# A hybrid two-layer trunk on one core: plain granules moved among the seven-product sets of its feed-forward parts

## The chip, the cores and the metric

The kernel runs on one core of a Trainium2 chip. The metric is the device time of one execution in microseconds (us); the kernel before took 1269.57 us, the median of three runs between 1269.21 and 1272.35. One core has a matrix engine (TensorE, PE in the profile), a vector engine (VectorE, DVE), a scalar engine (ScalarE, ACT), GpSimd (POOL) and SyncE (SP), which here issues loads. Each works through its own list of instructions in order; semaphores tie the lists together, and DMA queues bring the weights from memory.

## The reference

A trunk of two layers over 256 tokens of width 1024, in float32. What is computed, cut to what matters here:

```python
h = x
for i in range(2):
    h = h + 0.5 * swiglu(rmsnorm(h, ffn1_norm[i]), ffn1_w_gate[i], ffn1_w_up[i], ffn1_w_down[i])
    hn = rmsnorm(h, mix_norm[i])
    h = h + (diff_attention(hn, ...) if i == 0 else ssd_mixer(hn, ...))
    h = h + memory_cross_attention(rmsnorm(h, xa_norm[i]), mem, ...)
    h = h + 0.5 * swiglu(rmsnorm(h, ffn2_norm[i]), ffn2_w_gate[i], ffn2_w_up[i], ffn2_w_down[i])
return rmsnorm(h, final_norm)

def swiglu(h, w_gate, w_up, w_down):
    return (jax.nn.silu(h @ w_gate) * (h @ w_up)) @ w_down
```

The four `swiglu` calls are the feed-forward parts (FFNs); the change touches them alone. The gate and up weights are 1024 by 2816, the down weight 2816 by 1024. The attention of layer 0 needs tables of cosines and sines of the positions (the rope tables), which the kernel works out during the first FFN.

## The kernel before, in words

**Products.** Every float32 operand of a matmul is split into two parts, a rounded high part and the rest, and a product takes three matmuls: high by high, high by low, low by high. Lines 262, 263 and 264 are these three (`mm3`). An operand of weights is split one **granule** at a time, two rows of 128 by 512 columns: ACT casts the high part (`whi`, line 224), DVE subtracts to get the low part (`wlo`, line 225). Four buffers each hold `whi` and `wlo`. The weights come as tiles of 1 MB (4 times 128 rows by 512 columns) in eight buffers; their loads stand in SP's queue. Granules are split a fixed number of granules ahead of their use, so the order in which they are used is also the order of splits on ACT and DVE and of loads on SP.

**An FFN.** The hidden width of 2816 is cut into chunks of 512, numbered 0 to 4, and a half chunk 5. Chunk 0 and the half chunk (gate and up side by side, tiles named `gateup`) are plain products, and in the first FFN chunk 1 too. The others are **sets**: gate and up of a chunk, for both halves of the tokens, as seven products of sums in place of eight plain ones. With b11 and b21 the upper and lower half of the up weight of the chunk and b12 and b22 those of the gate, the seven are, in the order in which PE does them: x1 = b11 + b12, b11, x2 = x1 + b22, b22, x3 = b12 + b22, b21, x4 = x2 + b21. The sums x1 and x2 are made by DVE (`Sum`, line 203, one instruction over a whole tile); x3 and x4 by DMAs of POOL's queue that add into a tile. The left operands are sums of token blocks (`s_hi`, `s_lo`, made by lines 481 and 486 from `sraw`). The seven results are collected in three banks of PSUM, so a product that adds onto a bank must wait until the result before has been read or moved: line 830 (`c12`, its tile is named p) reads the bank that b22's product has filled, before x3's product may go on in it; line 835 (`c22`) does the like after b21's product, and line 841 takes the two products with the up results.

**Order.** A product is two granules, 6 matmuls each. Between the products stand **hosts**: plain granules of 12 matmuls (half chunk, plain chunks, down products of earlier chunks). The lists `five`, `six`, `eight` and `ten` say how many hosts stand ahead of each of the seven products of a set; `share` deals them out and `weave` makes the one list. After each chunk the hidden values are transposed by PE (line 854, `htp`) and split into `hid_hi` by ACT and `hid_lo` by DVE (line 858).

**The down product** has two halves of 512 output columns. Its `d0` and `d1` granules up to chunk 3 are hosts. What is left stands at the end: `d0[7:]`, of half 0 (chunk 3's second granule, chunk 4's two), then the tail of half 1 (chunks 3 and 4, two granules each). `fin` updates h with the finished half and starts the next norm. In the last FFN a function of its own (`last`) does the tail by token blocks, and half 0's evaluation goes with it. Up chunks end in line 804 (`up_fin`), which also calls what else hangs on that chunk: after chunk 1 of the first FFN the rope tables (lines 735 to 771, some forty small DVE instructions).

PE, DVE, ACT and SP follow the written order only for the first two units of the program; later a scheduler orders the lists, from the order in which the program names the work.

Of the kernel before, what the change touches and what calls it, by code (L numbers as in the profile page):

```python
# [57 lines left out]
def trunk(ctx, tc, a, out):  # L58
# [81 lines left out]
    pipe = Pipe()  # L140
    units = []
# [260 lines left out]
    def weave(steps):  # L402
        def run(*gr):
            for g, (_, f) in zip(use(gr), steps):
                f(g)
        units.append(([g for g, _ in steps], run))

    def down(src, half, ks, lhs, banks, first, last):

        def step(g):  # L410
            if not banks:
                banks.extend(acc("out") for _ in range(2))
            for k in range(g.nk):
                kt = g.k0 + k
                for t in range(2):
                    xh, xl = pipe.need(lhs, kt)
                    ts = slice(t * P, (t + 1) * P)
                    mm3(banks[t], xh[:, ts], xl[:, ts], g.hi[:, k, :], g.lo[:, k, :], kt == first, kt == end)
                    pipe.pe(0.68)
                if kt == end:  # L420
                    last(half, banks)
        end = ks[-1][0] + ks[-1][1] - 1 if last else -1
        return [(Gran(k, 2, (w, 0, 512)), step) for w in [W(src, k0, nk, half * 512, 512) for k0, nk in ks]
                for k in range(w.k0, w.k0 + w.nk, 2)]
# [350 lines left out]
        nc.scalar.activation(sin.rearrange("p t f -> p (t f)"), tot, AF.Sin)  # L775


    def ffn_hidden(nm, l, norm, fin, extra=None):
        hid = [None] * NHT
        box = {}  # L780

# [80 lines left out]
        wide([(wg, 0, 512)], norm, "gate", gate_fin(0), **({} if units else dict(single=True, eng=nc.gpsimd)))  # L862
        c = HID // 512
        half = stream([(wg, c * 512, 256), (wu, c * 512, 256)], norm, "gateup", up_fin(c, 256, 256))
        five, six = [1, 0, 1, 0, 1, 1, 1], [1, 1, 1, 0, 1, 1, 1]
        eight, ten = [2, 1, 1, 1, 1, 1, 1], [2, 1, 2, 1, 2, 1, 1]
        if norm is first_norm:
            wide([(wu, 0, 512)], norm, "up", up_fin(0))
            n = half + stream([(wg, 512, 512)], norm, "gate", gate_fin(1)) + stream([(wu, 512, 512)], norm, "up", up_fin(1))
            counts = {2: eight, 3: eight, 4: ten}  # L870
        else:
            n = stream([(wu, 0, 512)], norm, "up", up_fin(0)) + half
            counts = {1: six, 2: five, 3: six, 4: five}
        wd = a[nm + "_w_down"][l]
# [10 lines left out]
        steps = []  # L885
# [2 lines left out]
            steps += share(n[:sum(k)], s, k)  # L888
            n = n[sum(k):]
        assert not n  # L890
        weave(steps + d0[7:])
        return hid, wd

    def ffn(nm, l, norm, nxt, extra=None):
        fin = upd(0.5, nxt)
        hid, wd = ffn_hidden(nm, l, norm, fin, extra)
        weave(down(wd, 1, [(12, 4), (16, 4)], hid, [], 12, fin))


    def diff_attention(norm, nxt, kv):  # L900
# [627 lines left out]
    def last(norm):  # L1528
# [7 lines left out]
                nc.gpsimd.dma_start(fn[c], a["vec"][352 + c * 512:352 + (c + 1) * 512].partition_broadcast(P))  # L1536


        def mms(o, t, g, k, cs, kt, start, stop):
            xh, xl = pipe.need(hid, kt)  # L1540
            ts = slice(t * P, (t + 1) * P)
            mm3(o, xh[:, ts], xl[:, ts], g.hi[:, k, cs], g.lo[:, k, cs], start, stop)
            pipe.pe(0.68 * (cs.stop - cs.start) / 512)
# [33 lines left out]
        def first_half(half, banks):  # L1577
            for t in range(2):
                for q in range(2):
                    evac(banks[t][:, q * 256:(q + 1) * 256], t, q)  # L1580
        hid, wd = ffn_hidden("ffn2", 1, norm, first_half, {12: final_gain})
        banks = {}

        def run(*gr):
            ready(gr[-1].at + AHEAD)
            last_ = gr[-1].k0 + gr[-1].nk == 20
            for t, c0, c1 in [(0, 0, 512), (1, 0, 256), (1, 256, 512)]:
# [7 lines left out]
                if last_:  # L1595
                    for q in range((c1 - c0) // 256):
                        evac(b[:, q * 256:(q + 1) * 256], t, 2 + c0 // 256 + q)
        ws = [W(wd, k, 4, 512, 512) for k in (12, 16)]
        gr = [Gran(k, 2, (w, 0, 512)) for w in ws for k in (w.k0, w.k0 + 2)]
        units.append((gr[:1], run))  # L1600
        units.append((gr[1:], run))


# [71 lines left out]
```

## Time and profile before

| | |
|---|---|
| median of three runs (lowest to highest) | 1269.57 us (1269.21 to 1272.35) |
| the profiled execution's own time | 1269.06 us |
| its span | 1267.2 us |
| PE busy | 1251.8 us, 99% |
| DVE busy | 1057.7 us, 83% |
| ACT busy | 878.6 us, 69% |
| granted PE clock, mean over the span | 0.997 |
| DMA moved | 213 GB/s on average |

The span runs from the first to the last recorded instruction; the execution's own time has 1.9 us around it. Matmuls are pipelined: a row's own duration is longer than the distance between two starts, so the distance of starts tells how fast PE goes. A row of the timeline has the start, the time to the end of the last instruction of the row, the engine, the line, the operation, what it writes and reads, its shape and how often in a row; in brackets the idle time ahead of it and what ended that. A row of the windows has the window, its length, the busy time (and count) of PE, DVE, ACT, POOL and the weight loads in the order PE, weight load, DVE, ACT, POOL, then the granted clock, the share of DMA and GB/s.

### The profile page before, as it was taken

How to read it: one execution, taken by the hardware profiler on the slowest of the kernel's cores; microseconds unless marked ns; L12 is line 12 of the kernel's file. 1: busy time of each engine (PE TensorE's matmuls, PEld its weight loads, DVE VectorE, ACT ScalarE, POOL GpSimd, SP SyncE). 2: the span in 40 equal slices, each digit the busy share in tenths (PEclk: the TensorE clock that was granted, in tenths of full speed). 3: DMA queues.
4: the chain of work that ended last, by engine and by line, in shares of the span. 5: the costliest groups of instructions: out<-in, count | busy, mean ns of one | idle time of the engine just before them, and what ended most of it. 6: DMA issues, size and time to landing. Idle time of an engine off the chain costs nothing.

```text
span 1267.2 us, 18142 instructions
## 1 busy us (share of the span) xinstructions
PE 1251.8 (99%) x6751; PEld 1070.5 (84%) x6751; DVE 1057.7 (83%) x1451; ACT 878.6 (69%) x1394; POOL 161.6 (13%) x139
## 2 busy tenths in 40 slices
PE   9999999999999999999999999999999999999997
PEld 6788888788998888887878889999998898888886
DVE  6989777886787898888998976788999887899886
ACT  6676764686676876766776856777776766877773
POOL 1111002111100011000111000022222200011100
PEclk9999999999999999999999999999999999999999
DMA  9977975335786698985899976665544686489971
GB/s 333 277 234 204 352 242 167 133 123 159 208 243 167 169 257 254 265 284 167 235 229 257 281 263 195 207 199 167 178 155 134 170 247 186 162 235 266 259 221 34
DMA packets 158315, 269.79 MB, mean 213 GB/s; under 512 B 6889, under 2 KB 43410, under 8 KB 158226
## 3 DMA queue, kind: packets, MB, share of 16 engines
q1 hardware_dynamic: 137744, 229.75, 53.2%
q0 software_dynamic: 19744, 38.28, 17.9%
q8 instruction: 53, 0.87, 0.3%
q10 hardware_dynamic: 738, 0.59, 0.1%
q14 instruction: 36, 0.29, 0.1%
HBM read 267.52 MB, written 1.08 MB: 212 GB/s over the span
## 4 chain that ended last, share of the span: by engine, by line
PE 87%; DVE 7%; issue 2%; DMA 2%; ACT 2%; POOL 0%; POOLq 0%; DVEq 0%; ACTq 0%
PE out L264 9%; PE out L263 8%; PE out L262 8%; PE seven L262 8%; PE seven L263 7%; PE seven L264 7%; DVE wlo L225 3%; PE xs L264 2%; DMA w<-in_ffn_w_gate_dram 2%; PE xs L262 2%; PE xs L263 2%; PE mk L262 1%; PE xq L263 1%; PE mk L264 1%; PE xq L264 1%
## 5 line engine op out<-in xcount | busy, mean ns | idle before, releaser
L225 DVE TENSOR_TENSOR wlo<-w,whi 128x1024 fp32r<-128x1024 f32 (+2 forms) x532 | 642.4, 1219 | 141.6 <-ACT whi L224 131.6
L224 ACT CAST whi<-w 128x1024 fp32r<-128x1024 f32 (+2 forms) x534 | 552.6, 1041 | 270.5 <-PE out L264 104.0
L264 PE MATMUL out<-whi,hid_lo 128*128 128x512 f32 x336 | 131.2, 391 | 0.9 <-DVE hid_lo L858 0.9
L263 PE MATMUL out<-wlo,hid_hi 128*128 128x512 f32 x336 | 131.3, 391 | 0.0
L262 PE MATMUL out<-whi,hid_hi 128*128 128x512 f32 x336 | 130.8, 394 | 0.0
L262 PE MATMUL seven<-whi,s_hi 128*128 128x512 f32 x272 | 107.9, 397 | 1.8 <-DVE p L830 1.8
L263 PE MATMUL seven<-wlo,s_hi 128*128 128x512 f32 x272 | 106.1, 390 | 0.4 <-DVE wlo L225 0.4
L264 PE MATMUL seven<-whi,s_lo 128*128 128x512 f32 x272 | 106.1, 390 | 0.0
L203 DVE TENSOR_TENSOR w<-w 128x2048 f32<-128x2048 f32 x32 | 73.2, 2286 | 6.3 <-DMA w<-in_ffn_w_gate_dram 6.2
L264 PEld LDWEIGHTS out<-whi,hid_lo 128*128 128x128 f32 x336 | 63.0, 188 | 15.0 <-DVE hid_lo L858 2.0
L199 POOL DMA_DIRECT2D w<-in_ffn_w_up_dram x30 | 36.5, 1233 | 305.9 <-DVE wlo L225 304.8
L263 PEld LDWEIGHTS out<-wlo,hid_hi 128*128 128x128 f32 x336 | 63.1, 188 | 13.8 <-DVE wlo L225 1.2
L262 PEld LDWEIGHTS out<-whi,hid_hi 128*128 128x128 f32 x336 | 63.1, 188 | 12.5
L263 PE MATMUL seven<-wlo,xh 128*128 128x512 f32 x180 | 70.4, 391 | 1.9 <-DVE wlo L225 1.9
L264 PE MATMUL seven<-whi,xl 128*128 128x512 f32 x180 | 70.4, 391 | 0.0
L262 PE MATMUL seven<-whi,xh 128*128 128x512 f32 x180 | 70.3, 391 | 0.0
L199 POOL DMA_DIRECT2D w<-in_ffn_w_gate_dram x30 | 36.9, 1467 | 227.7 <-DVE w L203 98.4
L262 PEld LDWEIGHTS seven<-whi,s_hi 128*128 128x128 f32 x272 | 51.1, 188 | 13.7 <-DVE p L830 3.9
L264 PEld LDWEIGHTS seven<-whi,s_lo 128*128 128x128 f32 x272 | 51.1, 188 | 10.8
L263 PEld LDWEIGHTS seven<-wlo,s_hi 128*128 128x128 f32 x272 | 51.1, 188 | 10.4 <-DVE wlo L225 0.8
L263 PEld LDWEIGHTS seven<-wlo,xh 128*128 128x128 f32 x180 | 33.9, 189 | 9.4 <-DVE wlo L225 2.3
L264 PEld LDWEIGHTS seven<-whi,xl 128*128 128x128 f32 x180 | 33.9, 189 | 7.1
(397 smaller groups left out, 3020.3 us busy)
## 6 DMA issues: line engine op xcount, KB each, us to landing
w<-in_ffn_w_up_dram SPq DMA_DIRECT2D x40, 1024.0 KB, 5.4
w<-in_ffn_w_down_dram SPq DMA_DIRECT2D x40, 1024.0 KB, 9.1
w<-in_ffn_w_gate_dram SPq DMA_DIRECT2D x38, 1024.0 KB, 7.3
w<-in_ssd_w_in_dram SPq DMA_DIRECT2D x24, 1024.0 KB, 5.4
w<-in_xa_w_kv_dram SPq DMA_DIRECT2D x16, 1024.0 KB, 5.3
w<-in_ffn_w_gate_dram POOLq DMA_DIRECT2D x30, 512.0 KB, 9.2
w<-in_ffn_w_up_dram POOLq DMA_DIRECT2D x30, 512.0 KB, 7.6
w<-in_da_w_in_dram SPq DMA_DIRECT2D x12, 1024.0 KB, 5.1
```

The costliest lines, as they stand in the source:

```text
L199: nc.gpsimd.dma_start(self.t[:, k:k + 2, :], w.src[r0:r0 + 2 * P, w.c0:w.c0 + w.n] .rearrange("(k p) c -> p k c", p=P), accum_op=ALU.add)
L203: nc.vector.tensor_tensor(self.t, self.l.t, w.t, op=ALU.add)
L224: nc.scalar.copy(hv, src)
L225: self.eng.tensor_tensor(self.lo[:, :, o:o + n], src, hv.bitcast(F32), op=ALU.subtract)
L262: nc.tensor.matmul(o, lhsT=lh, rhs=rh, start=start, stop=False, skip_group_check=onto)
L263: nc.tensor.matmul(o, lhsT=lh, rhs=rl, start=False, stop=False, skip_group_check=onto)
L264: nc.tensor.matmul(o, lhsT=ll, rhs=rh, start=False, stop=stop, skip_group_check=onto)
```

## The change

Three things move; no computation is added or taken away. The counts of hosts ahead of the seven products change: in `five` and `six` the host that stood ahead of b21's product goes ahead of x3's, where there are two now. In the first FFN the three sets get counts of their own, 11, 8 and 7 hosts in place of 8, 8 and 10, and the first set starts behind five hosts in place of two. And the tail's first granule, of half 1, is put ahead of the two granules of chunk 4 of half 0, in all four FFNs; to that end the tail is handed into `ffn_hidden`, and `last` builds its list there.

```diff
--- before.py
+++ after.py
@@ -775,7 +775,7 @@
         nc.scalar.activation(sin.rearrange("p t f -> p (t f)"), tot, AF.Sin)
 
 
-    def ffn_hidden(nm, l, norm, fin, extra=None):
+    def ffn_hidden(nm, l, norm, fin, tail, extra=None):
         hid = [None] * NHT
         box = {}
 
@@ -862,12 +862,11 @@
         wide([(wg, 0, 512)], norm, "gate", gate_fin(0), **({} if units else dict(single=True, eng=nc.gpsimd)))
         c = HID // 512
         half = stream([(wg, c * 512, 256), (wu, c * 512, 256)], norm, "gateup", up_fin(c, 256, 256))
-        five, six = [1, 0, 1, 0, 1, 1, 1], [1, 1, 1, 0, 1, 1, 1]
-        eight, ten = [2, 1, 1, 1, 1, 1, 1], [2, 1, 2, 1, 2, 1, 1]
+        five, six = [1, 0, 1, 0, 2, 0, 1], [1, 1, 1, 0, 2, 0, 1]
         if norm is first_norm:
             wide([(wu, 0, 512)], norm, "up", up_fin(0))
             n = half + stream([(wg, 512, 512)], norm, "gate", gate_fin(1)) + stream([(wu, 512, 512)], norm, "up", up_fin(1))
-            counts = {2: eight, 3: eight, 4: ten}
+            counts = {2: [5, 1, 1, 0, 2, 1, 1], 3: [1, 1, 1, 1, 2, 1, 1], 4: [1, 1, 1, 0, 2, 1, 1]}
         else:
             n = stream([(wu, 0, 512)], norm, "up", up_fin(0)) + half
             counts = {1: six, 2: five, 3: six, 4: five}
@@ -888,13 +887,12 @@
             steps += share(n[:sum(k)], s, k)
             n = n[sum(k):]
         assert not n
-        weave(steps + d0[7:])
-        return hid, wd
+        tail = tail(hid, wd)
+        weave(steps + d0[7:9] + tail[:1] + d0[9:] + tail[1:])
 
     def ffn(nm, l, norm, nxt, extra=None):
         fin = upd(0.5, nxt)
-        hid, wd = ffn_hidden(nm, l, norm, fin, extra)
-        weave(down(wd, 1, [(12, 4), (16, 4)], hid, [], 12, fin))
+        ffn_hidden(nm, l, norm, fin, lambda hid, wd: down(wd, 1, [(12, 4), (16, 4)], hid, [], 12, fin), extra)
 
 
     def diff_attention(norm, nxt, kv):
@@ -1536,8 +1534,10 @@
                 nc.gpsimd.dma_start(fn[c], a["vec"][352 + c * 512:352 + (c + 1) * 512].partition_broadcast(P))
 
 
+        hid = []
+
         def mms(o, t, g, k, cs, kt, start, stop):
-            xh, xl = pipe.need(hid, kt)
+            xh, xl = pipe.need(hid[0], kt)
             ts = slice(t * P, (t + 1) * P)
             mm3(o, xh[:, ts], xl[:, ts], g.hi[:, k, cs], g.lo[:, k, cs], start, stop)
             pipe.pe(0.68 * (cs.stop - cs.start) / 512)
@@ -1578,8 +1578,7 @@
             for t in range(2):
                 for q in range(2):
                     evac(banks[t][:, q * 256:(q + 1) * 256], t, q)
-        hid, wd = ffn_hidden("ffn2", 1, norm, first_half, {12: final_gain})
-        banks = {}
+        banks, gr = {}, []
 
         def run(*gr):
             ready(gr[-1].at + AHEAD)
@@ -1595,9 +1594,12 @@
                 if last_:
                     for q in range((c1 - c0) // 256):
                         evac(b[:, q * 256:(q + 1) * 256], t, 2 + c0 // 256 + q)
-        ws = [W(wd, k, 4, 512, 512) for k in (12, 16)]
-        gr = [Gran(k, 2, (w, 0, 512)) for w in ws for k in (w.k0, w.k0 + 2)]
-        units.append((gr[:1], run))
+
+        def tail(hid_, wd):
+            hid.append(hid_)
+            gr.extend(Gran(k, 2, (w, 0, 512)) for w in [W(wd, k, 4, 512, 512) for k in (12, 16)] for k in (w.k0, w.k0 + 2))
+            return [(gr[0], run)]
+        ffn_hidden("ffn2", 1, norm, first_half, tail, {12: final_gain})
         units.append((gr[1:], run))
```

What moves is seen in the lists of DVE. A name's number tells tiles apart and differs between the kernels. First the first set of the first FFN, some 33 to 47 us into the span before. `w_442` is the Sum's tile (x1, then x2), `w_438` b11, `w_510` the half chunk's tile; before:

```order
L676 TENSOR_SCALAR cols0_96<-cols0_96 128x1
L203 TENSOR_TENSOR w_442<-w_438,w_440 128x2048
L481 TENSOR_TENSOR sraw_451<-sraw_414,y_263 128x256
L481 TENSOR_TENSOR sraw_451<-sraw_414,y_264 128x256
L481 TENSOR_TENSOR sraw_505<-y_261 128x256
L481 TENSOR_TENSOR sraw_505<-y_262 128x256
L225 TENSOR_TENSOR wlo_437<-w_442,whi_436 128x1024
L486 TENSOR_TENSOR s_lo_461<-sraw_451,s_hi_460 128x512
L225 TENSOR_TENSOR wlo_468<-w_442,whi_467 128x1024
L858 TENSOR_TENSOR hid_lo_480<-htp_474,hid_hi_479 128x512
L225 TENSOR_TENSOR wlo_509<-w_510,whi_508 128x1024
L858 TENSOR_TENSOR hid_lo_489<-htp_483,hid_hi_488 128x512
```

and now (`w_533` is the Sum's tile, `w_529` b11, `w_507` a host's):

```order
L225 TENSOR_TENSOR wlo_506<-w_507,whi_505 128x1024
L486 TENSOR_TENSOR s_lo_518<-sraw_502,s_hi_517 128x512
L203 TENSOR_TENSOR w_533<-w_529,w_531 128x2048
L804 SCALAR_TENSOR_TENSOR gs_549<-gateup_443,rcol_302,gs_549 128x256
L804 SCALAR_TENSOR_TENSOR gs_550<-gateup_444,rcol_302,gs_550 128x256
L225 TENSOR_TENSOR wlo_528<-w_533,whi_527 128x1024
L225 TENSOR_TENSOR wlo_556<-w_533,whi_555 128x1024
L225 TENSOR_TENSOR wlo_574<-w_507,whi_573 128x1024
L858 TENSOR_TENSOR hid_lo_587<-htp_581,hid_hi_586 128x512
L225 TENSOR_TENSOR wlo_594<-w_529,whi_593 128x1024
L203 TENSOR_TENSOR w_533<-w_533,w_603 128x2048
```

The x1 Sum stood ahead of both splits of its own and ahead of two `hid_lo`; now it comes behind the `s_lo` and the hosts' splits, with the half chunk's line 804 directly behind it, and x2's Sum has moved down with it.

Next set 2 of layer 0's second FFN, where line 830 reads the bank of b22's product. `w_4562` is x3's tile, `w_4706` and `w_4798` are hosts', `w_4770` (before) and `w_4776` (now) b21's; before:

```order
L225 TENSOR_TENSOR wlo_4705<-w_4706,whi_4704 128x1024
L203 TENSOR_TENSOR w_4855<-w_4851,w_4853 128x2048
L858 TENSOR_TENSOR hid_lo_4719<-htp_4713,hid_hi_4718 128x512
L225 TENSOR_TENSOR wlo_4726<-w_4562,whi_4725 128x1024
L225 TENSOR_TENSOR wlo_4736<-w_4562,whi_4735 128x1024
L830 TENSOR_TENSOR p2_4747<-p2_4747,seven_4639 128x512
L225 TENSOR_TENSOR wlo_4759<-w_4706,whi_4758 128x1024
L225 TENSOR_TENSOR wlo_4769<-w_4770,whi_4768 128x1024
L225 TENSOR_TENSOR wlo_4781<-w_4770,whi_4780 128x1024
L835 TENSOR_TENSOR p0_4646<-p0_4646,seven_4639 128x512
```

and now:

```order
L225 TENSOR_TENSOR wlo_4705<-w_4706,whi_4704 128x1024
L203 TENSOR_TENSOR w_4855<-w_4851,w_4853 128x2048
L858 TENSOR_TENSOR hid_lo_4719<-htp_4713,hid_hi_4718 128x512
L225 TENSOR_TENSOR wlo_4726<-w_4706,whi_4725 128x1024
L225 TENSOR_TENSOR wlo_4736<-w_4562,whi_4735 128x1024
L830 TENSOR_TENSOR p2_4747<-p2_4747,seven_4639 128x512
L225 TENSOR_TENSOR wlo_4759<-w_4562,whi_4758 128x1024
L225 TENSOR_TENSOR wlo_4775<-w_4776,whi_4774 128x1024
L225 TENSOR_TENSOR wlo_4787<-w_4776,whi_4786 128x1024
L225 TENSOR_TENSOR wlo_4797<-w_4798,whi_4796 128x1024
L835 TENSOR_TENSOR p0_4646<-p0_4646,seven_4639 128x512
```

Both splits of the hosts' `w_4706` now stand ahead of x3's two; before, one of them stood behind these. Line 830 is the sixth row in both, and line 835 has come to stand behind one more split, that of the next host.

Last the second set of the first FFN, set 3, where line 804 of up chunk 1 calls the rope tables. `w_849` is the Sum's tile there, `w_845` b11, `w_936` a host's; before, that place read:

```order
L225 TENSOR_TENSOR wlo_1006<-w_1007,whi_1005 128x1024
L804 SCALAR_TENSOR_TENSOR gs_775<-up_811,rcol_302,gs_775 128x512
L804 SCALAR_TENSOR_TENSOR gs_776<-up_812,rcol_302,gs_776 128x512
L735 CAST posf_954<-pos_98 128x2
L225 TENSOR_TENSOR wlo_1018<-w_889,whi_1017 128x1024
L738 TENSOR_SCALAR ang_953<-cst_93,posf_954 128x32 x2
L225 TENSOR_TENSOR wlo_1030<-w_889,whi_1029 128x1024
L747 TENSOR_SCALAR part_959<-ang_953 128x64
L225 TENSOR_TENSOR wlo_1066<-w_1007,whi_1065 128x1024
L749 TENSOR_TENSOR nrest_961<-ang_953,part_959 128x64
L754 TENSOR_SCALAR frac_963<-part_959 128x64
L858 TENSOR_TENSOR hid_lo_1044<-htp_1038,hid_hi_1043 128x512
```

and now:

```order
L804 SCALAR_TENSOR_TENSOR gs_732<-up_740,rcol_302,gs_732 128x512
L804 SCALAR_TENSOR_TENSOR gs_733<-up_741,rcol_302,gs_733 128x512
L735 CAST posf_883<-pos_98 128x2
L225 TENSOR_TENSOR wlo_948<-w_845,whi_947 128x1024
L738 TENSOR_SCALAR ang_882<-cst_93,posf_883 128x32 x2
L203 TENSOR_TENSOR w_849<-w_849,w_975 128x2048
L747 TENSOR_SCALAR part_888<-ang_882 128x64
L858 TENSOR_TENSOR hid_lo_960<-htp_954,hid_hi_959 128x512
L749 TENSOR_TENSOR nrest_890<-ang_882,part_888 128x64
L754 TENSOR_SCALAR frac_892<-part_888 128x64
L858 TENSOR_TENSOR hid_lo_969<-htp_963,hid_hi_968 128x512
L755 TENSOR_SCALAR whole_893<-frac_892 128x64
```

Before, three splits stood among the first small rope instructions and no Sum. Now the Sum of x2 (`w_849<-w_849,w_975`) and two `hid_lo` stand there, and the next split is two rows below the last row shown; between it and the split after that are 17 more small instructions and two more `hid_lo`.

## The prediction

> **What bounds the kernel now.** The page comes first: TensorE (PE) is busy for all but 15 us of the span. A change of order can win only from pauses of PE, so the second view is the list of who PE waited for, and the third the timeline around each such wait.
>
> ```profile
> PE 1251.8 (99%) x6751; PEld 1070.5 (84%) x6751; DVE 1057.7 (83%) x1451; ACT 878.6 (69%) x1394; POOL 161.6 (13%) x139
> PE seven L263 <- DVE wlo L225: 2.2, 2, 1.9
> PE seven L262 <- DVE p L830: 1.8, 3, 0.9
> PE out L264 <- DVE hid_lo L858: 0.9, 1, 0.9
> ```
>
> Read these as place, releaser, total, times, longest. All the releasers are VectorE (DVE) instructions of the feed-forward parts (FFNs). The pauses one by one, as PE's timeline has them:
>
> ```profile
> 31.27 0.48 PE L262 MATMUL gateup<-whi,xh 128*128 128x512 f32 x1
> 34.79 1.03 PE L854 MATMUL htp<-ident,gs 128*128 128x128 f32 x8
> 35.58 0.48 PE L262 MATMUL gateup<-whi,xh 128*128 128x512 f32 x1
> 37.72 0.39 PE L262 MATMUL seven<-whi,s_hi 128*128 128x512 f32 x1
> 38.46 0.50 PE L263 MATMUL seven<-wlo,s_hi 128*128 128x512 f32 x1 [0.36 <-DVE wlo L225]
> 45.71 0.61 PE L262 MATMUL gateup<-whi,xh 128*128 128x512 f32 x2
> 48.21 0.50 PE L263 MATMUL seven<-wlo,xh 128*128 128x512 f32 x1 [1.88 <-DVE wlo L225]
> 48.82 0.63 PE L262 MATMUL seven<-whi,xh 128*128 128x512 f32 x1
> 52.19 0.39 PE L263 MATMUL gateup<-wlo,xh 128*128 128x512 f32 x1
> 67.44 0.39 PE L262 MATMUL gate<-whi,xh 128*128 128x512 f32 x1
> 68.64 0.50 PE L263 MATMUL gate<-wlo,xh 128*128 128x512 f32 x1 [0.81 <-DVE wlo L225]
> 479.31 0.50 PE L262 MATMUL seven<-whi,s_hi 128*128 128x512 f32 x1 [0.46 <-DVE p L830]
> 571.82 0.50 PE L264 MATMUL out<-whi,hid_lo 128*128 128x512 f32 x1 [0.88 <-DVE hid_lo L858]
> 657.61 0.50 PE L262 MATMUL seven<-whi,s_hi 128*128 128x512 f32 x1 [0.88 <-DVE p L830]
> 1153.99 0.50 PE L262 MATMUL seven<-whi,s_hi 128*128 128x512 f32 x1 [0.46 <-DVE p L830]
> ```
>
> Undisturbed, a matmul starts 0.23 us after the one before (the pair at 45.71 lasts 0.61, one alone 0.39). The time lost at a pause is the distance of starts less 0.23; about 0.1 goes again at the matmul behind it. At 67.44: 1.20 - 0.23 + 0.11 = 1.08. So the bracketed idle plus 0.27 is the loss: 0.6 at 37.72, 1.1 at 67.44, 0.7, 1.15, 1.15 and 0.7 at the last four. The one behind 45.71 is dearer: the third start is due at 46.17 and comes at 48.21, 2.04 late, and the matmuls behind it last 0.63. From 48.21 to 52.19 there are ten distances, 3.98 us in place of 2.27: another 1.7. The windows say why:
>
> ```profile
> 48.00:49.00 1.00, 0.79 (x3) 0.66 (x4) 1.00 (x2) 0.52 (x1) 0.00 (x0) 0.85 0.03 4
> 50.00:51.00 1.00, 1.00 (x4) 0.72 (x4) 1.00 (x2) 0.66 (x2) 0.28 (x1) 0.50 0.92 309
> 60.00:70.00 10.00, 9.19 (x41) 7.30 (x40) 7.89 (x7) 7.47 (x9) 1.93 (x2) 1.00 0.71 230
> ```
>
> The granted clock (third from the end) was 0.50 after the 1.88 us pause, and 1.00 throughout the window of the 0.81 us one. In all: 0.6 + 3.7 + 1.1 + 0.7 + 1.15 + 1.15 + 0.7 = **9.1 us** that this change aims at.
>
> **First part, first set.** DVE works its list in order, and the Sums (L203) stand in front of splits that PE needs at once:
>
> ```profile
> 33.65 2.28 DVE L203 TENSOR_TENSOR w<-w 128x2048 f32<-128x2048 f32 x1
> 35.85 0.76 DVE L481 TENSOR_TENSOR sraw<-sraw,y 128x256 f32<-128x256 f32 x2
> 44.13 2.28 DVE L203 TENSOR_TENSOR w<-w 128x2048 f32<-128x2048 f32 x1
> 46.34 0.68 DVE L486 TENSOR_TENSOR s_lo<-sraw,s_hi 128x512 fp32r<-128x512 f32 x1
> 46.94 4.62 DVE L225 TENSOR_TENSOR wlo<-w,whi 128x1024 fp32r<-128x1024 f32 x4
> 65.16 2.29 DVE L203 TENSOR_TENSOR w<-w 128x2048 f32<-128x2048 f32 x1 [1.41 <-DMA w<-in_ffn_w_gate_dram]
> 52.85 0.48 ACT L787 ACTIVATE gs<-gateup,rcol 128x256 f32<-128x256 f32 x1 [0.97 <-PE gateup L264]
> 53.92 2.05 ACT L224 CAST whi<-w 128x1024 fp32r<-128x1024 f32 x2
> ```
>
> Started to started, a Sum is 2.2 us, a split (wlo) 1.14, an s_lo or hid_lo 0.60, an sraw 0.34, a cast 1.0. A host granule gives PE 12 matmuls (2.72), a product's granule 6 (1.36). With five hosts ahead PE has work from 31.3 for 5 x 2.72 and 0.8 of transposes (34.79 to 35.58), to 45.7. DVE from 33.65: three splits 3.4, three s_lo 1.8, two hid_lo 1.2, four sraw 1.35, so the Sum runs 41.4 to 43.6, two microseconds ahead of need. What decides is then the half-width gate: its last matmul falls at 31.3 + 4 x 2.72 + 0.8 = 43.0, ScalarE (ACT) takes two silu (0.95) and a cast (1.0), DVE a split (1.14): first product ready at 46.3, while PE, with one matmul and four transposes in between, is there at 46.2 to 46.4. I charge 0.3. The second Sum ends at 52.6, the split behind it at 53.75, and PE wants that at 53.8: 0.1. Below nothing it cannot go; if the silu is late, what it costs is its own delay. So 0.6 + 3.7 becomes 0.4. The pause at 67.44 came from a Sum that waited 1.41 us for its tile; now that tile takes b22's buffer, free (counted on in the same way) at about 59.5, and the Sum comes only at about 66. DMA prices:
>
> ```profile
> 30.00:40.00 10.00, 9.64 (x47) 7.49 (x45) 9.94 (x16) 3.98 (x7) 2.61 (x2) 1.00 1.05 384
> DMA to landing us min/median/max: 7.0/7.4/16.1
> ```
>
> (the second row is of the weight DMAs issued from 30 to 60 us). 59.5 + 7.4 = 66.9 at worst delays the Sum to 69 and the split behind it to 70.3; PE wants that at 71. I count the 1.1 as won. The queue SP carries the same tiles, one megabyte per 2.7 us at 384 GB/s, in another order; the half-width pairs and the gate tile needed first now come first.
>
> **Two hosts behind B22's product.** The product behind it starts on a bank that p (L830) must first read. Before, one host covered that (2.72 us); PE was 0.46 to 0.88 early. The second host adds 2.72, and p stands at the same place of DVE's list. No split is due earlier: the host's own moves up by two granules, the product's move back. The place given up, between that product and b21's, had 2.72 us more than needed: its reader L835 must be done before the last product, which still has b21 and a host, 5.4 us, in front. In set 1 of the three later FFNs the next Sum moves up ahead of b21's second split. From b22's end, DVE has the up projection's two L804 done at 4.3, then a split 5.4, the Sum 7.6, two hid_lo 8.8, the split 9.95; PE wants it after two hosts 5.44, three product granules 4.08, transposes 0.8 and one matmul 0.23, at 10.55. That holds while the Sum's tile is there in time; if not, it is a pause like that at 571.82. Won: 0.7 + 1.15 + 0.7 = 2.55.
>
> **A granule ahead of the last chunk's.** At 571.82 hid_lo stood behind a Sum waiting for its tile. Now the Sum stands behind both hid_lo, and PE has 2.72 us more. Against it, half 0 ends 2.72 later, with 8.2 us left to update h and transpose it. Two updates take 1.3 us after the last matmul, PE reaches the transposes 1.4 after: 0.1. In the last FFN the first half's evaluation, 4.05 us on DVE (1249.11 to 1253.16 in its timeline), ends as the next begins: 0.
>
> **What is new: the first FFN's second set (set 3).** In the first FFN the hosts shift, and the up projection now ends on the first host of set 3. Its rope tables then fall on the x2 Sum of that set, together with four hid_lo, where they stood singly between splits before:
>
> ```profile
> 96.83 1.40 DVE L804 SCALAR_TENSOR_TENSOR gs<-up,rcol,gs 128x512 f32<-128x512 f32 x2
> 98.22 1.22 DVE L225 TENSOR_TENSOR wlo<-w,whi 128x1024 fp32r<-128x1024 f32 x1
> 99.36 0.38 DVE L738 TENSOR_SCALAR ang<-cst,posf 128x32 f32<-128x32 f32 x2
> 102.16 0.19 DVE L754 TENSOR_SCALAR frac<-part 128x64 f32<-128x64 f32 x1
> 102.26 0.68 DVE L858 TENSOR_TENSOR hid_lo<-htp,hid_hi 128x512 fp32r<-128x512 f32 x1
> 103.66 0.22 DVE L756 TENSOR_TENSOR frac<-frac,whole 128x64 f32<-128x64 f32 x1
> 103.80 0.22 DVE L749 TENSOR_TENSOR nrest<-nrest,part 128x64 f32<-128x64 f32 x1
> ```
>
> Small ones are 0.10 to 0.14 each. Count from the end of the up projection. DVE: 0.2 to see it, L804 and posf 1.39, split 1.14, ang 0.3, Sum 2.2, five small ones and two hid_lo 1.75, split 1.14: 8.1. Then 17 small ones 2.05, two hid_lo 1.2, and wlo_1021 at 12.5; 12.9 if ACT's hid_hi hold it up. PE: x1 2.72, 16 transposes 1.6, a host 2.72, b11 2.72, then five matmuls of later granules 1.15: 10.9. The matmul that needs wlo_1021 stands 1.6 to 2.0 us; I take **1.8**, about 95 us into the span. Behind it all splits have 1.14 against 1.36 or more.
>
> Does the clock drop there too? PE's idle comes in two pieces, about 1.2 (a cast of the third granule ahead) and 0.6, between the 0.88 that cost no clock and the 1.88 that cost 1.7. I take nothing, and keep 1.7 for the range. [...]
>
> **Sum.** -9.1 + 0.4 + 0.1 + 1.8 = -6.8 us. The profiled execution took 1269.06 (span 1267.2 and 1.9 around it), so 1262.3; the median of the runs shown is 0.5 above it: **1262.7 us**.
>
> **Rivals.** (A) The same, but clock lost at 95 us and a first product a little later: +1.7 to 2.5, 1264.4 to 1265.2. For it: the same idle total as at 48 us. (B) The change does not do in the first part what it says: the pauses there only move behind the silu and the rope tables. Then only the later FFNs' 2.55 + 1.05 count: 1266.0. For it, the 0.1 us margins; against, the Sum's two. (C) The rope tables cost nothing since DVE is ahead: 1260.9. Against it: L804 cannot start before the up projection ends. (D) Slower: the Sum of set 4's x1, now ahead of b21's splits of set 3, waits for its tile, asked for near 105 and wanted near 113. It decides from 10.4 us of landing on; at the 16.1 of the row PE stands 5.7 and loses two stretches of clock, 3.4: +2.3, 1271.9, and more with a second late tile. Against it: the median of 7.4.
>
> **Chances.** Forecast 0.46, A 0.20, B 0.16, C 0.10, D 0.08. What a measurement tells from no change is 0.3%, 3.8 us: faster is below 1265.8, slower above 1273.4. Forecast, A, C and a third of B are faster, less some for what is uncounted: 0.74; slower half of D: 0.04; the rest 0.22. C and the lower end of the rope cost set the low bound, 1260.3; B with a clock loss the high one, 1267.6.
>
> **What would show it.** Right: no PE wait on p (L830) or hid_lo, none of over 0.5 us between 36 and 70, granted clock 1.00 from 40 to 60, and one wait on wlo near 95 of 1 to 2 us. Wrong: a wait longer than 0.5 near 46 (the silu), a clock of 0.50 at 95 to 100 (A), DVE idle on a DMA ahead of L203 near 113 (D), or no wait at 95 (C).

## The result and the profile after

| | before | changed |
|---|---|---|
| median (lowest to highest), four runs each | 1269.67 us (1269.21 to 1272.35) | 1260.69 us (1260.51 to 1261.86) |
| ratio, 95% interval | | 0.9927 (0.9910 to 0.9944) |
| profiled execution's own time | 1269.06 | 1260.69 |
| its span | 1267.2 | 1258.9 |

The change is faster by 9.0 us in the medians and by 8.4 between the two profiled executions; 6.8 were forecast. The time of 1260.69 lies in the range on record, 2.0 below the point and 0.4 above the range's lower end.

The list of who PE waited for, in the changed kernel (place, releaser, total, times, longest), without the warm-up at the start:

```profile
PE out L262 <- ACT whi L224: 0.5, 1, 0.5
PE seven L262 <- ACT p L823: 0.4, 1, 0.4
PE out L263 <- DVE wlo L225: 0.3, 1, 0.3
```

These are the three longest; the other rows are of 0.3 us or less. The waits on p (L830) and on hid_lo are gone, and none of those on wlo near 38, 46 and 67 us is left. The three rows shown lie within 3 us of each other, at 95 us on PE's timeline; the first three rows here are from the place of the old wait near 46:

```profile
45.33 0.39 PE L262 MATMUL seven<-whi,s_hi 128*128 128x512 f32 x1
45.56 0.60 PE L854 MATMUL htp<-ident,gs 128*128 128x128 f32 x4
45.91 0.48 PE L263 MATMUL seven<-wlo,s_hi 128*128 128x512 f32 x1
...
94.05 0.61 PE L262 MATMUL out<-whi,hid_hi 128*128 128x512 f32 x2
95.02 0.49 PE L262 MATMUL seven<-whi,s_hi 128*128 128x512 f32 x1 [0.35 <-ACT p L823]
95.96 0.73 PE L262 MATMUL out<-whi,hid_hi 128*128 128x512 f32 x2 [0.45 <-ACT whi L224]
96.98 0.50 PE L263 MATMUL out<-wlo,hid_hi 128*128 128x512 f32 x1 [0.29 <-DVE wlo L225]
```

At 45.91 the first product's low matmul starts on time. From 94.27 (the second of the two matmuls in the row of 94.05) to 96.98 the distances of starts add up to 1.91 us more than the usual ones: this is the stall that the prediction put at about 95 us with 1.8. The windows show that the clock did not drop at either place (the last three columns are the granted clock, the share of DMA and GB/s):

```profile
40.00:50.00 10.00, 10.00 (x48) 8.26 (x47) 9.61 (x11) 7.52 (x10) 2.61 (x2) 1.00 0.82 212
94.49:97.90 3.41, 2.32 (x8) 1.27 (x8) 3.41 (x11) 1.42 (x2) 0.00 (x0) 1.00 0.76 283
```

And VectorE's timeline at the places that the steps of the prediction name:

```profile
40.85 2.28 DVE L203 TENSOR_TENSOR w<-w 128x2048 f32<-128x2048 f32 x1
...
44.31 3.49 DVE L225 TENSOR_TENSOR wlo<-w,whi 128x1024 fp32r<-128x1024 f32 x3 [0.39 <-ACT whi L224]
...
67.10 2.29 DVE L203 TENSOR_TENSOR w<-w 128x2048 f32<-128x2048 f32 x1 [1.97 <-DMA w<-in_ffn_w_gate_dram]
...
95.71 1.22 DVE L225 TENSOR_TENSOR wlo<-w,whi 128x1024 fp32r<-128x1024 f32 x1
...
113.87 2.29 DVE L203 TENSOR_TENSOR w<-w 128x2048 f32<-128x2048 f32 x1 [1.65 <-DMA w<-in_ffn_w_gate_dram]
...
563.61 1.29 DVE L858 TENSOR_TENSOR hid_lo<-htp,hid_hi 128x512 fp32r<-128x512 f32 x2 [0.79 <-ACT hid_hi L857]
564.82 2.28 DVE L203 TENSOR_TENSOR w<-w 128x2048 f32<-128x2048 f32 x1
```

Two of these Sums still wait, 1.97 and 1.65 us, for a tile. PE loses 0.11 us behind the first and nothing behind the second; at 564 the Sum stands behind both hid_lo.

Below, "lost" always means distances of PE's starts beyond the usual ones, added up over a place. By that count the execution before lost 23.7 us in all and the changed one 15.4; the difference, 8.3, is the whole difference of the spans.

### The profile page after: what moved, and what is told of

Same layout as the page of the kernel before. It is cut to its first block, busy times and chain, and to the rows that moved or that the text cites. A ratio compares the mean times of both kernels' runs of the same rounds, so it can differ in the third digit from the quotient of the medians.

```text
span 1258.9 us, 18179 instructions
## 1 busy us (share of the span) xinstructions
PE 1248.6 (99%) x6751; PEld 1070.7 (85%) x6751; DVE 1056.7 (84%) x1451; ACT 878.0 (70%) x1395; POOL 161.7 (13%) x139
## 3 DMA queue, kind: packets, MB, share of 16 engines
HBM read 267.52 MB, written 1.08 MB: 213 GB/s over the span
## 4 chain that ended last, share of the span: by engine, by line
PE 91%; DVE 4%; DMA 2%; ACT 1%; issue 1%; POOL 0%; POOLq 0%; DVEq 0%; ACTq 0%
PE out L263 9%; PE out L264 8%; PE out L262 8%; PE seven L264 8%; PE seven L263 8%; PE seven L262 8%; DVE wlo L225 2%; PE xs L264 2%; PE xs L262 1%; PE xs L263 1%; DMA w<-in_ffn_w_gate_dram 1%; PE up L263 1%; PE up L264 1%; PE up L262 1%; PE htp L854 1%; PE mk L262 1%
## 5 line engine op out<-in xcount | busy, mean ns | idle before, releaser
L262 PEld LDWEIGHTS seven<-whi,xh 128*128 128x128 f32 x180 | 33.8, 188 | 7.1
```

What stands on the lines that cost most here:

```text
L262: nc.tensor.matmul(o, lhsT=lh, rhs=rh, start=start, stop=False, skip_group_check=onto)
```

## The experiments

Every run stands beside runs of the kernel before on the same chip; its median there was 1269.55 in the first group of four, 1270.21 in the second and 1272.04 (seven runs) in the last.

### The parts alone

The first kernel is the one before with the new lists alone:

```diff
-        five, six = [1, 0, 1, 0, 1, 1, 1], [1, 1, 1, 0, 1, 1, 1]
+        five, six = [1, 0, 1, 0, 2, 0, 1], [1, 1, 1, 0, 2, 0, 1]
```

> The kernel before with the new lists five and six alone (two hosts ahead of x3's product, none ahead of b21's; the first FFN and the tails as before). Theory (the pauses on p are PE being 0.5 to 0.9 us early, and 2.72 us more of other work covers them): the waits on p, L830, near 478, 656 and 1153 us go and nothing comes in their place, so -2.6 to -2.9 us against the kernel before (0.73 + 1.15 + 0.73 and 0.11 at the matmul behind each). Rival (the pause only moves, to b21's split behind the Sum or to L835, where a host less stands): 0 to -1 us, with new waits on wlo or p within 10 us of the old places.

Measured: 1264.82 us, ratio 0.9968 (0.9958 to 0.9978), so -4.7 in the medians. No wait on p is left, as the theory has it, but in the profiled execution one place has a new pause: near 478.8 us PE loses 0.5 on wlo, behind a Sum that waited 1.21 us for its tile. The gain is larger than 2.9 all the same, because the wait on hid_lo near 571 us went too. Its VectorE timeline there:

```profile
568.75 1.29 DVE L858 TENSOR_TENSOR hid_lo<-htp,hid_hi 128x512 fp32r<-128x512 f32 x2 [0.79 <-ACT hid_hi L857]
569.96 2.28 DVE L203 TENSOR_TENSOR w<-w 128x2048 f32<-128x2048 f32 x1
```

The scheduler, given only the new lists, had already put the Sum behind both hid_lo. The tail's granule, to which the prediction gave that gain, is not needed for it.

The second has the tail's granule alone (the changed kernel with the old counts everywhere):

```diff
-        five, six = [1, 0, 1, 0, 2, 0, 1], [1, 1, 1, 0, 2, 0, 1]
+        five, six = [1, 0, 1, 0, 1, 1, 1], [1, 1, 1, 0, 1, 1, 1]
-            counts = {2: [5, 1, 1, 0, 2, 1, 1], 3: [1, 1, 1, 1, 2, 1, 1], 4: [1, 1, 1, 0, 2, 1, 1]}
+            counts = {2: [2, 1, 1, 1, 1, 1, 1], 3: [2, 1, 1, 1, 1, 1, 1], 4: [2, 1, 2, 1, 2, 1, 1]}
```

> The kernel before with the tail's first granule alone put ahead of the last chunk of half 0, in all four FFNs. Theory: the wait on hid_lo near 571 us goes, -1.05 to -1.15 us; the granule that half 0 ends later costs 0.1 or nothing at the three boundaries and at the end. Rival (half 0's end sets the start of the next part, so that a granule is paid there): 0 us or slower, with PE idle at the ends of the FFNs.

Measured: 1267.17 us, ratio 0.9992 (0.9978 to 1.0006): -2.4 by the medians, and not told from nothing by the interval. In its profile the wait on hid_lo is gone and the three on p are there, with 0.73 lost at each.

The third has the first FFN's counts alone:

```diff
-            counts = {2: eight, 3: eight, 4: ten}
+            counts = {2: [5, 1, 1, 0, 2, 1, 1], 3: [1, 1, 1, 1, 2, 1, 1], 4: [1, 1, 1, 0, 2, 1, 1]}
```

> The kernel before with the new counts of the first FFN alone (11, 8 and 7 hosts, five of them ahead of set 2). Theory: the waits at 38, 46 and 67 us and the stretch of half clock go (0.81 + 2.04 + 1.66 + 1.08 = 5.6), a stall of 1.9 us comes at 95 us: -3.7 us, and with e1 and e2 a sum of -7.4 to -7.8. Rival (part of the gain in the changed kernel came from somewhere else, the sum of the three edits is not the whole): this one alone gains 5 or more, or the three fall short of the whole 9.0 by more than 1.5.

Measured: 1264.45 us, ratio 0.9963 (0.9953 to 0.9973), -5.1, where 3.7 were expected. By the median the rival's 5 is met; the interval, 3.4 to 6.0 us less, holds the expected 3.7 as well. In the first FFN the profile shows what was expected: nothing lost at 38 and 46 us, 0.53 at 70, 1.88 at 95. This profiled execution was the slowest of its ten (1268.2; the others 1263.3 to 1265.0), and its waits say why; the first row is of the list of PE's waits:

```profile
PE out L264 <- DVE hid_lo L858: 2.7, 1, 2.7
```

The second is of VectorE's timeline:

```profile
566.94 2.29 DVE L203 TENSOR_TENSOR w<-w 128x2048 f32<-128x2048 f32 x1 [2.60 <-DMA w<-in_ffn_w_gate_dram]
```

The Sum ahead of hid_lo waited 2.60 us for its tile here, 0.83 in the profiled execution of the kernel before: with the old order at the tail, the length of that pause is a matter of when one transfer lands. Together the three parts give 12.2 us and the whole 9.0. One cause is shown: the first two both take the pause at the tail away, so it is counted twice, at 1.2 to 2.8 us and, in the third kernel's profile, 1.55 of half clock besides. What is left of the difference lies within the intervals of the three.

The changed kernel once more:

> The changed kernel once more, beside the kernel before. The three edits alone gave -4.7, -2.4 and -5.1 us (medians), 12.2 together, where the whole gave 9.0. Theory (executions differ by a late tile and by whether a pause costs a stretch of half clock, so parts and whole agree only within some 3 us): again 1260 to 1262, -8 to -10. Rival (the first four executions of the changed kernel were slow ones, and the whole is the sum): 1257.5 to 1259, -11 or more.

Measured: 1261.38 us (1260.51 to 1261.87), ratio 0.9929 (0.9916 to 0.9942), and 1.91 us lost at 94 us again. The whole is 9, not 12.

### The stall at 95 us: the rope tables moved

```diff
-            {1: param_cols, 3: rope_tables, 5: lam_col, 12: mem_stage} if l == 0 else {12: kvs[1].prep})
+            {1: param_cols, 9: rope_tables, 5: lam_col, 12: mem_stage} if l == 0 else {12: kvs[1].prep})
```

> The changed kernel with the rope tables hung on the end of the first FFN's last set (set 4) in place of its chunk 1. Theory (the stall near 95 us comes of the rope tables' small instructions bunched with the x2 Sum and four hid_lo on VectorE): it goes whole, -1.9 us against the changed kernel, 1258.8 us, and nothing comes near 150 us, where only plain granules follow. Rival (ScalarE is the bound there, with the exponential's table load of 1.28 us and its casts, since the profile names its p and whi as releasers): at least 0.8 us of the stall stays, 1259.6 or more.

Measured: 1260.46 us (1259.73 to 1263.74), ratio 0.9941 (0.9923 to 0.9960). The stall went whole: nothing of 0.1 us or more is lost between 20 and 112 us. By its time alone the rival's 1259.6 or more is met, but ScalarE's table load for the exponential (1.28 us, at 85.36 in the changed kernel) was left where it was and the stall is gone, so the rival falls: p and whi, named as releasers, were late because of VectorE's list. The time hardly moved, since a new pause came. PE's timeline:

```profile
112.73 0.39 PE L262 MATMUL out<-whi,hid_hi 128*128 128x512 f32 x1
115.03 0.74 PE L263 MATMUL out<-wlo,hid_hi 128*128 128x512 f32 x1 [1.91 <-DVE wlo L225]
```

VectorE's timeline:

```profile
105.64 0.68 DVE L830 TENSOR_TENSOR p<-p,seven 128x512 f32<-128x512 f32 x1
106.34 1.23 DVE L225 TENSOR_TENSOR wlo<-w,whi 128x1024 fp32r<-128x1024 f32 x1
111.54 2.29 DVE L203 TENSOR_TENSOR w<-w 128x2048 f32<-128x2048 f32 x1 [3.98 <-DMA w<-in_ffn_w_gate_dram]
```

And the windows around it:

```profile
111.70:115.12 3.42, 1.51 (x8) 0.93 (x6) 3.42 (x3) 1.97 (x2) 0.68 (x1) 1.00 0.14 51
115.12:118.53 3.41, 3.41 (x8) 2.67 (x9) 3.41 (x4) 0.66 (x1) 1.77 (x2) 0.50 0.70 178
```

This is the mechanism of rival D of the prediction, at its place: the Sum of set 4's x1 waited 4.0 us for its tile (asked for at 101.67, landed at 111.42), and the splits behind it came late. PE waited for the first of them, that of the host ahead of b21's product. It costs 2.07 us and, in this execution, 1.70 more at half clock. (The profiled execution is the slowest of the four, 1263.74; the others took 1259.73 to 1260.81. It also lost 1.2 us near 1149, behind another Sum that waited 1.89 for its tile.)

In the changed kernel the same Sum waits 1.65 us and PE loses nothing. One could think that the stall at 95 made PE come late enough not to notice, but the traces show another cause. The changed kernel's VectorE timeline there:

```profile
109.24 0.68 DVE L830 TENSOR_TENSOR p<-p,seven 128x512 f32<-128x512 f32 x1
109.84 2.39 DVE L225 TENSOR_TENSOR wlo<-w,whi 128x1024 fp32r<-128x1024 f32 x2
113.87 2.29 DVE L203 TENSOR_TENSOR w<-w 128x2048 f32<-128x2048 f32 x1 [1.65 <-DMA w<-in_ffn_w_gate_dram]
```

and PE's, at the same matmul of that host:

```profile
115.27 0.39 PE L263 MATMUL out<-wlo,hid_hi 128*128 128x512 f32 x1
```

Here two splits stand between line 830 and the Sum, with late rope tables only one: the host's split has come to stand behind the Sum. PE's lateness does not help, since the tile comes as much later: the host's first matmul starts 1.3 us behind the landing in both (112.73 behind 111.42, and 115.04 behind 113.75). An estimate from the changed kernel's times says the same: with the other order its host's split would end at 117.2, two microseconds after PE wanted it at 115.27. So the scheduler, with the rope tables gone from there, put this Sum one split earlier, and that gave the gain back. Late rope tables with the Sum in exactly its old place were not run.

### The Sum behind the splits

On top of the late rope tables, one Sum is kept in the program's order (60 is the count of granules split when the program comes to it):

```diff
-                nc.vector.tensor_tensor(self.t, self.l.t, w.t, op=ALU.add)
+                add = nc.vector.tensor_tensor(self.t, self.l.t, w.t, op=ALU.add)
+                if self.into is None and done[0] == 60:
+                    tc.keep_in_program_order(add)
```

> The changed kernel with the rope tables at the end of set 4 and with set 4's x1 Sum kept in the program's order on VectorE, behind b21's splits of set 3 and x4's. Theory (what the late rope tables won was given back because that Sum, waiting 4.0 us for its tile, stood ahead of b21's split: rival D's mechanism): no pause of PE near 95 or 113 us, no half clock there; 0.5 to 2 us less than with the rope tables moved alone (1260.5), and 1.5 to 2.5 less than the changed kernel: 1258.3 to 1259.5. Rival (PE then waits for x1's own split, right behind the Sum, near 127 us): a pause there of 1 us or more and no gain.

Measured: 1258.46 us (1258.26 to 1259.11), ratio 0.9908 (0.9893 to 0.9922): 2.9 less than the changed kernel beside it, and the fastest kernel here. The stall is 1.9 of that; the rest was not followed up. Its VectorE timeline at that Sum:

```profile
120.25 1.22 DVE L227 TENSOR_TENSOR wlo<-w,whi 128x1024 fp32r<-128x1024 f32 x1
121.38 2.28 DVE L203 TENSOR_TENSOR w<-w 128x2048 f32<-128x2048 f32 x1
```

The Sum now starts at 121.38, ten microseconds later than in the kernel above, without a wait, and PE has none near 95, 113 or 127 us. All that its list of waits still holds behind the warm-up is:

```profile
PE qkt L940 <- POOL rt L931: 0.2, 1, 0.2
PE acs L1277 <- PE mk L266: 0.2, 1, 0.2
```

The Sum's place alone, with the rope tables where the change put them:

> The changed kernel with only set 4's x1 Sum kept behind b21's and x4's splits; the rope tables where the change put them. Theory (the Sum's wait is covered in the changed kernel, since PE comes 1.9 us later there): the stall of 1.9 us at 95 us stays, nothing else moves, 1260.4 to 1261.4, the same as the changed kernel. Rival (the Sum's place alone carries the gain of 2.9 seen with both): 1259.3 or less.

Measured: 1260.85 us (1260.77 to 1261.04), ratio 0.9920 (0.9894 to 0.9946), with 1.90 lost at 94 us: the same as the changed kernel, in which that Sum's wait had cost nothing. The gain takes both edits.

### How much room the two placements had

Four hosts ahead of the first set, in place of five:

```diff
-            counts = {2: [5, 1, 1, 0, 2, 1, 1],
+            counts = {2: [4, 2, 1, 0, 2, 1, 1],
```

> The changed kernel with four hosts ahead of the first set in place of five, the fifth put ahead of b11's product. Theory (the margin of the first product was a few tenths: its split ended near 45.4, PE wanted it at 45.6): PE comes 2.72 us sooner and stands 1.4 us (if the Sum binds) to 2.6 us (if the half chunk's silu binds) near 43 us, so +1.4 to +2.6 against the changed kernel, and 1.7 more where that costs a stretch of half clock. Rival (there was spare time of a host or more): 0.5 or less.

Measured: 1263.91 us (1263.72 to 1265.58), ratio 0.9953 (0.9937 to 0.9968), 2.5 over the changed kernel beside it. PE's timeline of the slowest of the four executions, the profiled one:

```profile
43.44 0.49 PE L262 MATMUL seven<-whi,s_hi 128*128 128x512 f32 x1 [0.82 <-ACT whi L224]
44.70 0.53 PE L263 MATMUL seven<-wlo,s_hi 128*128 128x512 f32 x1 [0.77 <-DVE wlo L225]
45.04 0.62 PE L264 MATMUL seven<-whi,s_lo 128*128 128x512 f32 x1
```

Its windows:

```profile
41.62:45.03 3.41, 1.82 (x7) 0.98 (x6) 2.32 (x4) 3.05 (x5) 2.55 (x2) 1.00 0.96 263
45.03:48.45 3.42, 3.42 (x10) 2.67 (x9) 3.42 (x5) 2.60 (x3) 0.00 (x0) 0.50 1.11 198
```

Two pauses lose 0.98 and 1.03 us and 1.6 go at half clock behind them, 3.7 in all. The other three executions, at a mean clock of 0.999 against 0.997 here, took 1263.72 to 1263.98, 1.7 less. So five hosts cover the chain, and four do not.

Two of the tail's granules ahead of half 0's last chunk (shown in part; `last` is changed to the same end):

```diff
-        weave(steps + d0[7:9] + tail[:1] + d0[9:] + tail[1:])
+        weave(steps + d0[7:9] + tail[:2] + d0[9:] + tail[2:])
```

> The changed kernel with two of the tail's granules ahead of the last chunk of half 0 in place of one; 5.4 us of work are then left behind half 0's end in place of 8.2. Theory (the update takes 1.3 us and PE reaches the transposes after the rest): still covered at the three boundaries, 0 to +1 us in all, the last FFN's evaluation of 4.05 us included. Rival (half 0's end sets when the next part can begin): +1 or more at each of the four ends, +4.

Measured: 1262.16 us (1261.63 to 1262.91), ratio 0.9937 (0.9919 to 0.9954), 0.8 over the changed kernel beside it, which the intervals do not tell apart. The profile places a cost all the same, at the very end. PE's last matmul and VectorE's last instruction of this kernel:

```profile
1251.94 0.28 PE L264 MATMUL fin<-whi,hid_lo 128*128 128x256 f32 x1
...
1256.20 0.35 DVE L1574 TENSOR_SCALAR h<-h,fss 128x256 f32<-128x256 f32 x1
```

VectorE ends 4.6 us behind the last matmul's start, in the changed kernel 2.9: the first half's evaluation is no longer covered, +1.7. At the other three ends nothing is lost.

### The clock: pauses of different length

In the version with both edits, the subtraction of 13 splits is repeated:

```diff
+AGAIN = {170 + 26 * i: 5 + i % 4 for i in range(13)}
...
-                self.eng.tensor_tensor(self.lo[:, :, o:o + n], src, hv.bitcast(F32), op=ALU.subtract)
+                for _ in range(AGAIN.get(self.at, 1)):
+                    self.eng.tensor_tensor(self.lo[:, :, o:o + n], src, hv.bitcast(F32), op=ALU.subtract)
```

> The version with the late rope tables and the Sum behind, where at 13 granules from 300 us on the split's subtraction on VectorE is repeated 5 to 8 times, so that PE stands there for different lengths; nothing else, the result is the same. Theory (PE's time is cut into windows of 3.413 us that run on from the first one, and a window in which PE lost about 2.0 us or more, 2.07 being the least seen to do it and 1.92 the most seen not to, is followed by one at half clock): each planned pause that puts 2.07 us or more into one window is followed by a half-clock stretch that begins at that window's end; a pause of 2 to 3.8 us that a window's edge cuts into pieces below 1.92 costs nothing further. Rival (the length of the pause decides): every pause over 2.07 us is followed by half clock, wherever it lies. Second rival (only a window in which PE does nothing at all counts): none under 3.4 us is.

Measured: 1324.85 us in one execution. The trace's clock records give every half-clock stretch but the one that the end cuts as 3.413 or 6.827 us long, each beginning a whole number of 3.413 us behind the first full clock (8.96 us here: 483.41 is 139 of them later, 596.05 is 172). Counted off in windows of 3.413 us from there, six at full clock lost 2.31, 2.31, 2.49, 2.93, 3.41 and 3.41 us, and each was followed by half clock; of the others the greatest lost 1.90, 1.88 and 1.85, and none was. Two of them and the windows behind:

```profile
592.63:596.05 3.42, 1.43 (x10) 0.89 (x8) 3.42 (x5) 3.28 (x8) 0.00 (x0) 1.00 0.00 0
596.05:599.46 3.41, 0.10 (x1) 0.10 (x1) 3.41 (x5) 0.54 (x2) 0.00 (x0) 0.50 0.00 0
...
715.51:718.93 3.42, 1.79 (x8) 1.16 (x7) 3.06 (x4) 3.10 (x5) 0.00 (x0) 1.00 1.00 240
718.93:722.34 3.41, 3.41 (x16) 2.81 (x15) 1.83 (x3) 2.20 (x4) 0.00 (x0) 1.00 1.10 265
```

PE's timeline at the first of them:

```profile
594.43 0.87 PE L539 MATMUL xt<-ident,h 128*128 128x128 f32 x6 [1.24 <-DVE h L589]
599.36 0.79 PE L267 MATMUL gate<-wlo,xh 128*128 128x512 f32 x1 [4.06 <-DVE wlo L229]
```

The half clock began at 596.05, when the pause that began near 595.3 had lasted less than 1 us and the one before it 1.24; the two lay in one window, of which PE was busy for 1.43 us. The other side, a longer pause that falls into two windows, did not come up in this run; the kernel with the new lists alone has it:

```profile
45.08 0.61 PE L262 MATMUL gateup<-whi,xh 128*128 128x512 f32 x2
47.59 0.50 PE L263 MATMUL seven<-wlo,xh 128*128 128x512 f32 x1 [1.90 <-DVE wlo L225]
```

Its windows there:

```profile
43.49:46.90 3.41, 2.20 (x10) 1.50 (x8) 3.41 (x4) 1.73 (x4) 0.00 (x0) 1.00 0.86 166
46.90:50.32 3.42, 2.73 (x12) 2.21 (x13) 3.42 (x4) 2.26 (x4) 0.21 (x1) 1.00 0.48 121
```

The pause is the one for which the kernel before paid 1.66 us of half clock (2.06 lost against 2.04); here the windows, counted off in the same way, meet at 46.90, which leaves 1.37 in the first, and both rows are at 1.00. The same execution has a longer one, at the Sum near 65 us, whose tile came later than in the kernel before (3.10 us of waiting against 1.41, with the same list there). PE's timeline:

```profile
65.23 0.39 PE L262 MATMUL gate<-whi,xh 128*128 128x512 f32 x1
68.13 0.50 PE L263 MATMUL gate<-wlo,xh 128*128 128x512 f32 x1 [2.51 <-DVE wlo L225]
```

Its windows:

```profile
63.97:67.38 3.41, 1.65 (x8) 1.03 (x6) 2.73 (x2) 2.10 (x2) 0.00 (x0) 1.00 0.57 220
67.38:70.80 3.42, 2.67 (x11) 2.17 (x12) 3.42 (x4) 0.00 (x0) 2.44 (x2) 1.00 0.36 47
```

It loses 2.67 us, well over 2.07, of which 1.92 fall into the window that ends at 67.38, and the next one is at 1.00. So, in these executions, the rival, by which the length of the pause decides, is out from both sides; the second rival, by which only a wholly idle window counts, is out by the four windows that lost 2.31 to 2.93.

## Why the prediction was right

**The pauses that go.** By starts the execution before lost 0.81, 2.04, 1.66 (half clock), 1.08, 0.73, 1.16, 1.15 and 0.73 us at the eight places, 9.4 where the prediction read 9.1; the first was read as 0.6. All are gone, and 0.11 at 70.58 us is what is left.

**First set.** Right in mechanism, and the residue of 0.4 was too much. The Sum ran 40.85 to 43.05, half a microsecond ahead of the forecast's 41.4 to 43.6. The gate's silu did decide, but the split behind it ended at 45.45 (44.31 and 1.14) in place of 46.3, and PE, through its four transposes, wanted it at 45.91: 0.46 to spare and nothing lost. (The terms that the prediction lists, from 43.0 on, add up to 46.1 and not to 46.3.) The silu decided by a hair: ScalarE was free for the cast at 43.24, and the Sum ended at about 43.1. With one host fewer PE stands there for 2.0 us, so the room is a fraction of a host.

**The Sum that waits for its tile (67 us).** Right, and narrow. It started at 67.10 after 1.97 us of waiting, about the worst case that the prediction still called won; 0.11 us were lost at the split behind it, 0.53 in the third kernel above.

**Two hosts.** Right: the three waits on p went, in the whole and alone, and the changed kernel has no pause in their place. The condition that the prediction set, that a Sum's tile be there in time, is a real one: behind a late Sum near these places PE lost 0.5 us in the kernel with the new lists alone (near 479) and 1.2 in the one with late rope tables (near 1149).

**The tail.** Right that the pause goes, wrong on what takes it away: the step gave it to the granule, and the new lists alone do it, by moving the Sum in the scheduler's order. That the granule costs nothing at the ends holds for one, and not for two.

**The rope tables.** Right in place and size: 1.91 us (1.91, 1.88, 1.90 in other executions) for 1.8. The sign on record was one wait on wlo; the trace has three short ones, on p, whi and wlo, all of which go with the tables. The last split of the bunch ended at 96.84, 12.6 us behind the up projection's end, where 12.5 were counted. So rival C is out. Rival A, half clock there, is out in all executions profiled with this stall: its window lost 1.91 us at most, and 1.2 to 1.7 in the others. It was a near thing: in the changed kernel the whole stall fell into one window, and 1.91 is 0.16 short of the least that was followed by half clock in any run here. The prediction's ground, that the idle time comes in two pieces of 1.2 and 0.6, does not account for it: with four hosts two pieces of 0.98 and 1.03 in one window were followed by half clock.

**Rival D** was given 0.08, and its cost did not come in the changed kernel. Its sign did: VectorE stood 1.65 us idle for the tile ahead of the Sum at 113.87. The landing took 9.2 us, and b21's first split ended at 117.22, 0.8 before PE wanted it. In the changed kernel's second profile the landing took 9.8 and 0.1 was left, so the 10.4 from which it was said to decide was about right, and the Sum's wait nearly cost something. With late rope tables 9.75 us were enough for a pause of 2.07, because there a host's split, needed sooner than b21's, stood behind the Sum too.

**The size.** Forecast -6.8, measured -8.3 between the spans. Of the 1.5 us, 0.3 is the misread sum of the pauses and 0.4 the residues of 0.4 and 0.1 that came out as 0.1; against it stands 0.1 for the stall. Some 0.5 is the first 20 us, where PE waits for the first tiles and no instruction was changed (2.4 lost before, 1.9 after in these executions), so it is chance; the rest, under half a microsecond, is scattered in pieces of 0.1 that were not followed up. The point itself should by its own terms have read 1262.8 for 1262.7. The medians are 9.0 apart, and the executions before are spread (1266.7 to 1273.1 over 24 of them). Two causes of spread are in the traces of the parts, though not shown for every execution: the late Sum near 568 us waits longer or shorter (2.60 us against 0.83), and the pause at 46 us is followed by half clock, 1.66 more, in the kernel before and by none in the kernel with the new lists alone.

## What to carry to other kernels

When instructions are moved and a scheduler orders the lists, read the list again behind the place that they left. Here, with the rope tables gone, an instruction that waits for a late tile came to stand one split earlier, and the 1.9 us won were given back; only the two edits together paid. VectorE worked through its list in order here: with late rope tables the Sum waited 3.98 us for its tile, and the split behind it, for which PE then waited 1.91 us, came late. Put such an instruction behind what is needed sooner, here ten microseconds later at no cost. When costing a pause, read the granted clock behind it too, and not the pause's length alone: two pauses of 0.98 and 1.03 us within 3.41 us were followed by 1.6 us lost at half clock here, and one of 2.06 us, in the kernel with the new lists alone, by none.

## What the runs showed of the hardware

PE's first full clock began 4.33 us into the span in the kernel before, at 5.74 in the changed one and at 8.96 in the run of different pauses. The one half-clock stretch in the middle of the kernel before lasted 3.413 us, from 48.71 to 52.12; those in the run of different pauses 3.413 or 6.827, but for the last, which the end closes. They began whole numbers of 3.413 us behind the first full clock: 13 in the kernel before (369 for its last, at 1263.85), 366 in the changed one (its only one, at 1255.02), 139 and 172 in the run of different pauses. Counted off in windows of that length, these losses of PE at full clock were followed by a window at 0.50: 2.15 us in the kernel before and in the one with the tail's granule alone, 2.07 with the late rope tables, 2.12 with four hosts, 2.55 with the first FFN's counts alone, and 2.31 to 3.41 six times in the run of different pauses. The greatest that were not are 1.92 (the kernel with the new lists alone, out of a pause of 2.67), 1.91 (the changed kernel) and 1.90 (the run of different pauses). What sets the clock was not shown. At half clock, 1.5 to 1.8 us went in each stretch of 3.413 into which no pause reached.
